# Gate projections with 512-column products, the dt step in four pieces, and a changed order of the output turns in a two-layer hybrid encoder

## The chip, the cores and the metric

One core of a Trainium2 chip runs the whole kernel. The metric is the device time of one execution in microseconds (us). The kernel before takes 1551.32 us (median of 3 runs, 1548.27 to 1552.07).

## The reference

Two layers work on 512 tokens of width 1024. Each layer is a mixer (a Mamba-2 state-space part beside windowed attention), an output projection, and a gated convolutional FFN. What the change touches:

```python
h = rms_norm(x, norm1_w[i])
proj = h @ w_in[i]
z, xbc, dt_raw, q, k, v = split(proj, ...)      # z: 1024 columns, 512 for each of 2 groups
dt = softplus(dt_raw + dt_bias[i])              # (L, 2 directions, 16 heads)
a_dt = dt * -exp(a_log[i])
a_cum = cumsum(a_dt)                            # inside each chunk of 128 tokens
decay = exp(a_cum[l] - a_cum[s])                # for l >= s; the other direction likewise
y_ssm = y_fwd + y_bwd + d_skip * xs
y_ssm = rms_norm(y_ssm * silu(z))               # per group of 512 columns
x = x + concat(y_ssm, y_attn) @ w_out[i]
```

All is fp32. The kernel splits each fp32 operand of a large product into a high and a low part (fp32r) and runs three products for one: high by high, high by low, low by high.

## The kernel before

Every large weight comes in units of up to 128 x 1024 elements. The list of units (L170 to L205) is the order of use. For each unit a DMA on the queue of SP fills one of 3 `raw` buffers (L141), ScalarE (ACT) copies the high part into one of 3 `whi` buffers (L161), and VectorE (DVE) subtracts it to give `wlo` (L162). `take` (L114) hands out a unit, and asks with high priority for the splits of three units ahead and the loads behind those. A `whi` buffer comes free when the last product that reads it is done.

One large product is three matmuls in `mm3` (L278 to L280). They write to 4 "dense" PSUM banks (`pd`, L98). Smaller products and transposes use 4 "small" banks (`psm`, L101). A planner orders the instructions of each engine when the program is built: it takes them in program order where they are ready by its own estimate of time, lets a later one go first on an engine that has nothing earlier ready, and puts `take` ahead. At run time each engine keeps that fixed order and waits on semaphores.

A layer's mixer goes as follows.

- **V and dt** (`vdt`, L496): 288 columns, into `v_sb` and `xdt`. The first layer's start (L509 to L538) is in an order written out by hand. The constants' transposes follow (`setup`, L266).
- **The dt step** (`dt_step`, L544, called at L610): the softplus as a chain of small VectorE instructions of 128 x 128 elements (L553 to L568), twelve products for the running sums (L581), their exponential `ex` (L582), a logarithm and an exponential on ScalarE (L586, L587), the copies `run` (L592), `own` (L593, L596), four transposes of `run` (L599), their copy (L601), a DMA to `sums` in DRAM (L602), and `sd` (L603, L604). Its tiles lie in a pool of their own that closes behind it (L611).
- **K** (L628), then ten dense pieces (L981): the state inputs `bc`, the queries `q`, the inputs `xa` and `xb`. `x_done` and `bc_done` run a convolution of 7 taps over two dense banks (L389, L395). Attention steps are mixed in between by `Side` (L400): each yield of a dense piece adds a credit, and a whole credit runs one step.
- **The gate** (`g_z`, L832, called for both groups at L993 and L994): per half of 256 columns it takes two units at once (4 contraction tiles each), and for each pair of token tiles fills one dense bank with 48 matmuls of 256 columns, then one Silu (L848) and a yield. That is 4 yields a group, and 192 matmuls.
- **The state-space steps** (`ssd_steps`, L853): 11 steps and 4 turns a group. A step fetches rows of `sums` by a DMA from POOL's queue (L898, 3 `rows` buffers), updates states (L875 to L882), forms decays on ScalarE and VectorE (L906 to L911), and multiplies (L922, L937). `outer` multiplies the result by `sz`, the gate. A turn scales and transposes one chunk (L955 to L962). The first group's steps and turns are mixed into the gate and the output projection, then the second group's.
- **The output projection** (`g_out`, L1008): two halves of 512 columns. It takes all 4 dense banks at once, and one unit (2 contraction tiles by 512 columns) per yield. The first group's turns must stand ahead of its unit 4.

Of the kernel before, what the change touches and what calls it, by code (L numbers as in the profile page):

```python
# [7 lines left out]
F32 = mybir.dt.float32  # L8
F32R = mybir.dt.float32r
AF = mybir.ActivationFunctionType  # L10
# [36 lines left out]
def encoder_kernel(  # L47
# [30 lines left out]
    def pool(name, **kw):  # L78
        return tc.tile_pool(name=name, **kw)
# [13 lines left out]
    def nm(s):  # L93
        uid[0] += 1
        return f"{s}_{uid[0]}"
# [74 lines left out]
    for i in range(DEPTH):  # L170
# [17 lines left out]
        for g in range(GROUPS):  # L188
            for half in range(2):
                pair(f"z{g}{half}", [(512 * g + 256 * half, 256)])  # L190
# [279 lines left out]
    for i in range(DEPTH):  # L470
        side = Side()
        with ExitStack() as mix:
# [17 lines left out]
            dtx = ExitStack()  # L490
            dtp = dtx.enter_context(pool(f"dt_{i}", bufs=1, reuse_waits="tile"))
            run = dtp.tile([P, NT, 2, 16], F32, name=nm("run"))
            xdt = dtp.tile([P, NT, 32], F32, name=nm("xdt"))
# [49 lines left out]

            def dt_step():  # L544

                def et(name, shape, dt=F32):
                    return dtp.tile([P] + shape, dt, name=nm(name))

                sp_e = et("sp_e", [NT, 32])
                sp_w = et("sp_w", [NT, 32])  # L550
                sp_w2 = et("sp_w2", [NT, 32])
                sp_a = et("sp_a", [NT, 32])
# [7 lines left out]
                for n in (15, 13, 11, 9, 7, 5, 3):  # L560
# [4 lines left out]


                adt = sp_e
                V.scalar_tensor_tensor(  # L568
                    adt,
# [5 lines left out]
                )  # L575
                ps = small_bank()
                cum = ps[:, : 6 * 64].rearrange("p (n c h) -> p n c h", n=6, c=NT)
                for n, (m, o) in enumerate(
                    ((f(t_le), 0), (f(t_gt), 0), (f(t_ge), 16), (f(t_lt), 16), (ones, 0), (ones, 16))
                ):  # L580
                    mm(cum[:, n], m, adt[:, :, o : o + 16], start=True, stop=True)  # L581
                S.activation(ex, cum, AF.Exp)  # L582

# [6 lines left out]

                for d in range(2):
                    S.copy(run[:, :, d], cum[:, 2 * d])  # L592
# [4 lines left out]
                psr = small_bank()  # L597
                for c in range(NT):
                    turn128(psr[:32, c * P : (c + 1) * P], run[:, c].rearrange("p d h -> p (d h)"), ident)  # L599
                runT = dtp.tile([32, NT, P], F32, name=nm("runT"))  # L600
                V.tensor_copy(runT, psr[:32].rearrange("p (c l) -> p c l", c=NT))  # L601
                nc.gpsimd.dma_start(sums[i].rearrange("c r l -> r c l"), runT)  # L602
                V.tensor_tensor(sd[:, 0], ex[:, 1], dts[:, :, 0:16], ALU.mult)  # L603
                V.tensor_tensor(sd[:, 1], ex[:, 3], dts[:, :, 16:32], ALU.mult)  # L604
# [6 lines left out]
            dtx.close()  # L611
# [147 lines left out]
            def xbc(g, r):  # L759
# [16 lines left out]
                def bc_turn():  # L776
# [55 lines left out]
            def g_z(g, r):  # L832
                sz = act_tile(F32)
                r["sz"] = sz
                for half in range(2):
                    ws = [take((i, f"z{g}{half}", j)) for j in range(2)]
                    cs = slice(256 * half, 256 * half + 256)
                    for tp in range(2):
                        bank = dense_bank()
                        for t in (2 * tp, 2 * tp + 1):  # L840
                            o = bank[:, (t % 2) * 256 : (t % 2) * 256 + 256]
                            sl = slice(t * P, (t + 1) * P)
                            for kt in range(KT):
                                hv, lv = (w.rearrange("p (k c) -> p k c", k=4)[:, kt % 4] for w in ws[kt // 4])
                                ah, al = hT[kt // 4]
                                mm3(o, ah[:, kt % 4, sl], al[:, kt % 4, sl], hv, lv, kt == 0, kt == KT - 1)
                        flush()
                        S.activation(sz[:, 2 * tp : 2 * tp + 2, cs], bank.rearrange("p (t c) -> p t c", t=2), AF.Silu)  # L848
                        yield
# [3 lines left out]
            def ssd_steps(sp, g, r):  # L853
# [123 lines left out]
                return [lambda k=k: step(k) for k in range(-1, 10)] + [lambda c=c: turn(c) for c in range(NT)]  # L977
# [14 lines left out]
            side.steps += ssd_steps(sp, 0, r0)  # L992
# [10 lines left out]
            side.steps += ssd_steps(sp, 1, r1)  # L1003
# [151 lines left out]
```

## Time and profile before

| | |
|---|---|
| median of 3 runs | 1551.32 us |
| profiled execution | 1550.66 us |
| span of the profile | 1549.0 us |
| TensorE (PE) busy | 1508.9 us, 97% |
| VectorE (DVE) busy | 876.5 us, 57% |
| ScalarE (ACT) busy | 793.4 us, 51% |
| GpSimd (POOL) busy | 174.7 us, 11% |
| mean granted clock of TensorE | 0.994 |

A busy PE counts each matmul from its start to its modelled end, and neighbours overlap, so the start-to-start distance tells what one costs. A row of the timeline has start, duration, engine, line, operation, written tile and read tiles, shapes, count, and in brackets the idle time before it with what ended that. A row of the windows has, for a stretch, the busy time of PE, weight loads (PEld), DVE, ACT and POOL with the number of instructions, then the granted clock, the DMA share and GB/s.

### The profile page before, as it was taken

What the parts mean: (1) busy time and instruction counts of PE and PEld (TensorE: products, weight loads), DVE (VectorE), ACT (ScalarE), POOL (GpSimd) and SP (SyncE); (2) the same over time, 40 slices, a digit from 0 to 9 for tenths busy, and PEclk for the clock granted to TensorE, in tenths of its full rate; (3) what the DMA queues carried; (4) which work ended last, traced back from release to release, by engine and by line L of the source; (5) the groups of instructions that cost most, each with busy time, mean ns of one, the idle gap of its engine ahead of it and who ended that gap; (6) DMA issues with size and microseconds to landing.
All of it is one profiled execution on the core that took longest, in us unless ns stands there. A gap on an engine that the chain in (4) does not pass through costs nothing.

```text
span 1549.0 us, 20219 instructions
## 1 busy us (share of the span) xinstructions
PE 1508.9 (97%) x7680; PEld 1238.0 (80%) x7680; DVE 876.5 (57%) x1406; ACT 793.4 (51%) x1464; POOL 174.7 (11%) x246
## 2 busy tenths in 40 slices
PE   7999999999999999999999999999999999999997
PEld 5787778877788888888887777887778888888886
DVE  5676777776644444433367777777666434443333
ACT  4467988863543233322356779788435323332223
POOL 2000002423200000000010000053232000000002
PEclk9899999999999999999999999999999999999999
DMA  6532333453323333322343322355422333333231
GB/s 206 156 82 76 83 85 103 134 169 95 108 88 98 102 95 96 95 96 95 99 137 104 89 75 62 83 123 182 132 95 82 95 97 101 101 96 96 95 96 68
DMA packets 113080, 161.48 MB, mean 104 GB/s; under 512 B 7932, under 2 KB 90108, under 8 KB 112975
## 3 DMA queue, kind: packets, MB, share of 16 engines
q1 hardware_dynamic: 104756, 132.60, 27.7%
q0 software_dynamic: 7648, 27.50, 6.7%
q8 instruction: 60, 0.98, 0.3%
q14 instruction: 38, 0.30, 0.1%
q10 hardware_dynamic: 578, 0.10, 0.0%
HBM read 155.82 MB, written 8.55 MB: 106 GB/s over the span
## 4 chain that ended last, share of the span: by engine, by line
PE 86%; ACT 4%; DVE 3%; issue 3%; POOL 2%; DMA 2%; POOLq 0%; ACTq 0%; DVEq 0%
PE pd L280 22%; PE pd L278 22%; PE pd L279 22%; PE psm L278 3%; PE psm L279 3%; PE psm L280 3%; PE psm L690 2%; PE psm L680 2%; PE psm L922 1%; PE psm L646 1%; DMA rows<-sums 1%; PE psm L647 1%; PE psm L937 1%; ACT whi L161 1%; PE psm L314 1%
## 5 line engine op out<-in xcount | busy, mean ns | idle before, releaser
L278 PE MATMUL pd<-t,whi 128*128 128x512 f32 (+1 forms) x1088 | 419.5, 386 | 1.5 <-ACT whi L161 1.5
L280 PE MATMUL pd<-t,wlo 128*128 128x512 f32 (+1 forms) x1088 | 419.4, 386 | 0.4 <-DVE wlo L162 0.4
L279 PE MATMUL pd<-t,whi 128*128 128x512 f32 (+1 forms) x1088 | 418.9, 385 | 0.0
L162 DVE TENSOR_TENSOR wlo<-raw,whi 128x1024 fp32r<-128x1024 f32 (+1 forms) x214 | 260.5, 1221 | 241.3 <-ACT whi L161 241.0
L161 ACT CAST whi<-raw 128x1024 fp32r<-128x1024 f32 (+1 forms) x214 | 221.8, 1040 | 240.9 <-PE pd L279 213.6
L278 PEld LDWEIGHTS pd<-t,whi 128*128 128x128 f32 x1088 | 204.7, 188 | 40.8 <-ACT whi L161 1.7
L280 PEld LDWEIGHTS pd<-t,wlo 128*128 128x128 f32 x1088 | 204.7, 188 | 40.2 <-issue 1.5
L279 PEld LDWEIGHTS pd<-t,whi 128*128 128x128 f32 x1088 | 205.0, 188 | 38.3 <-issue 0.8
L278 PE MATMUL pd<-whi,t 128*128 128x256 f32 (+2 forms) x544 | 188.9, 347 | 0.0
L279 PE MATMUL pd<-wlo,t 128*128 128x256 f32 (+2 forms) x544 | 180.3, 331 | 4.0 <-DVE wlo L162 3.9
L280 PE MATMUL pd<-whi,t 128*128 128x256 f32 (+2 forms) x544 | 181.7, 334 | 0.7 <-DVE t L962 0.7
L279 PEld LDWEIGHTS pd<-wlo,t 128*128 128x128 f32 x544 | 103.9, 191 | 17.2 <-DVE wlo L162 4.6
L278 PEld LDWEIGHTS pd<-whi,t 128*128 128x128 f32 x544 | 103.9, 191 | 13.7 <-issue 3.8
L280 PEld LDWEIGHTS pd<-whi,t 128*128 128x128 f32 x544 | 103.8, 191 | 11.5 <-DVE t L962 1.6
L1097 ACT CAST ph<-t 128x512 fp32r<-128x512 f32 x40 | 24.9, 623 | 143.0 <-PE psm L279 132.5
L1098 DVE TENSOR_TENSOR pl<-t,ph 128x512 fp32r<-128x512 f32 x40 | 27.7, 692 | 114.8 <-ACT ph L1097 114.8
L395 DVE SCALAR_TENSOR_TENSOR sg<-pd,fprm,sg 128x511 f32<-128x511 f32 x88 | 65.9, 748 | 30.7 <-ACT sg L389 29.0
L648 DVE CUSTOM_DVE_ANT_0 s<-psm,bias,sink_all 128x256 f32<-128x256 f32 (+1 forms) x128 | 65.6, 547 | 21.2 <-PE psm L647 8.0
L662 ACT ACTIVATE s<-s,nm 128x257 f32<-128x257 f32 (+1 forms) x128 | 70.5, 554 | 3.3 <-DVE nm L659 3.1
L395 DVE SCALAR_TENSOR_TENSOR xT<-pd,cprm,xT 128x511 f32<-128x511 f32 (+2 forms) x96 | 66.6, 742 | 5.2 <-PE psm L680 4.3
L278 PE MATMUL pd<-whi,ph 128*128 128x512 f32 x176 | 68.9, 391 | 0.0
L279 PE MATMUL pd<-wlo,ph 128*128 128x512 f32 x176 | 68.7, 390 | 0.0
(205 smaller groups left out, 2181.1 us busy)
## 6 DMA issues: line engine op xcount, KB each, us to landing
raw<-in_w_up_dram SPq DMA_DIRECT2D x88, 512.0 KB
raw<-in_w_in_dram SPq DMA_DIRECT2D x52, 512.0 KB
raw<-in_w_down_dram SPq DMA_DIRECT2D x44, 512.0 KB
rows<-sums POOLq DMA_DIRECT2D x32, 512.0 KB, 5.8
raw<-in_w_out_dram SPq DMA_DIRECT2D x32, 512.0 KB
bias<-toep POOLq DMA_DIRECT2D x16, 384.0 KB, 4.0
raw<-in_w_in_dram SPq DMA_DIRECT2D x18, 256.0 KB
x<-in_x_dram SPq DMA_DIRECT2D x8, 512.0 KB
```

The source lines that it names most:

```text
L161: S.copy(hi[:, :used], raw[:, :used])
L162: V.tensor_tensor(lo[:, :used], raw[:, :used], f(hi[:, :used]), ALU.subtract)
L278: mm(o, lh, rh, start=start, stop=False)
L279: mm(o, lh, rl, start=False, stop=False)
L280: mm(o, ll, rh, start=False, stop=stop)
L395: V.scalar_tensor_tensor(dst[:, lo:hi], src[:, lo + d : hi + d], taps[k], dst[:, lo:hi], ALU.mult, ALU.add)
L648: V.tensor_tensor_reduce(out=s4[:, h, :w], in0=ps[:, :w], in1=it.bias[h // 2][:, h % 2, it.j0 : it.j1], scale=1.0, scalar=sink4[:, h : h + 1],
L662: S.activation(s4[:, h, : w + 1], s4[:, h, : w + 1], AF.Exp, bias=nm4[:, h : h + 1], accum_out=den[:, h : h + 1])
L680: turn128(ps[:, c : c + P], it.s4[:, h, b * P : (b + 1) * P], ident)
L690: mm(po[c * HD : (c + 1) * HD, :256], v_sb[:, it.k0 // P + b, it.g * HD : (it.g + 1) * HD], it.pts[b][:, c * 256 : (c + 1) * 256], start=( ...
L1097: S.copy(h, p_sb[kt])
L1098: V.tensor_tensor(l, p_sb[kt], f(h), ALU.subtract)
```

## The change

The gate's units become 2 contraction tiles by 512 columns, four of them a group. `g_z` takes all 4 dense banks, one unit per yield, and issues 24 matmuls of 512 columns per yield; the four Silus follow in the last of the four. There are still 4 yields a group, so every credit falls as before. The dt step keeps only the chain up to L568 where it was. The rest is cut into `dt_sums` (called behind the first query piece), `dt_rows` (behind the second) and `dt_own` (behind the third). Its tiles move into the mixer's pool, and the scratch tile `junk` has one buffer in place of two. `ssd_steps` returns steps and turns apart, and the first group's four turns stand one place later, behind the second group's first step, which holds one fetch of rows and nothing else.

```diff
-            for half in range(2):
-                pair(f"z{g}{half}", [(512 * g + 256 * half, 256)])
+            for j in range(4):
+                add_unit((i, f"z{g}", j), wi, 2 * j, 2, [(512 * g, 512)])
...
-            dtp = dtx.enter_context(pool(f"dt_{i}", bufs=1, reuse_waits="tile"))
-            run = dtp.tile([P, NT, 2, 16], F32, name=nm("run"))
+            run = ep.tile([P, NT, 2, 16], F32, name=nm("run"))
...
+            def dt_sums():
+                ps = small_bank()
+                cum = ps[:, : 6 * 64].rearrange("p (n c h) -> p n c h", n=6, c=NT)
...
+                    mm(cum[:, n], m, sp_e[:, :, o : o + 16], start=True, stop=True)
+                S.activation(ex, cum, AF.Exp)
+                for d in range(2):
+                    S.copy(run[:, :, d], cum[:, 2 * d])
+                V.tensor_tensor(sd[:, 0], ex[:, 1], dts[:, :, 0:16], ALU.mult)
+                V.tensor_tensor(sd[:, 1], ex[:, 3], dts[:, :, 16:32], ALU.mult)
+
+            def dt_rows():
+                psr = small_bank()
+                for c in range(NT):
+                    turn128(psr[:32, c * P : (c + 1) * P], run[:, c].rearrange("p d h -> p (d h)"), ident)
+                runT = ep.tile([32, NT, P], F32, name=nm("runT"))
+                V.tensor_copy(runT, psr[:32].rearrange("p (c l) -> p c l", c=NT))
+                nc.gpsimd.dma_start(sums[i].rearrange("c r l -> r c l"), runT)
+
+            def dt_own():
                 V.tensor_scalar(sp_w, dts, 1e-37, None, ALU.max)
...
-                        junk = ep.tile([P, P], F32, tag="junk", name=nm("junk"), bufs=2)
+                        junk = ep.tile([P, P], F32, tag="junk", name=nm("junk"), bufs=1)
...
-                for half in range(2):
-                    ws = [take((i, f"z{g}{half}", j)) for j in range(2)]
-                    cs = slice(256 * half, 256 * half + 256)
-                    for tp in range(2):
-                        bank = dense_bank()
...
-                        S.activation(sz[:, 2 * tp : 2 * tp + 2, cs], bank.rearrange("p (t c) -> p t c", t=2), AF.Silu)
-                        yield
+                banks = [dense_bank() for _ in range(NT)]
+                for j in range(4):
+                    hi, lo = take((i, f"z{g}", j))
...
+                    for t in range(NT):
+                        sl = slice(t * P, (t + 1) * P)
+                        for k in range(2):
+                            kt = 2 * j + k
+                            ah, al = hT[kt // 4]
+                            mm3(banks[t], ah[:, kt % 4, sl], al[:, kt % 4, sl], hv[:, k], lv[:, k], kt == 0, kt == KT - 1)
+                        if j == 3:
+                            S.activation(sz[:, t], banks[t], AF.Silu)
+                    flush()
+                    yield
...
-                return [lambda k=k: step(k) for k in range(-1, 10)] + [lambda c=c: turn(c) for c in range(NT)]
+                return [lambda k=k: step(k) for k in range(-1, 10)], [lambda c=c: turn(c) for c in range(NT)]
...
+            later = {1: dt_sums, 3: dt_rows, 5: dt_own}
             for n, gen in enumerate(dense):
                 side.run(gen, RATE_A if n > 1 else 0)
+                if n in later:
+                    later[n]()
...
-            side.steps += ssd_steps(sp, 1, r1)
+            steps1, turns1 = ssd_steps(sp, 1, r1)
+            side.steps += steps1[:1] + turns0 + steps1[1:] + turns1
```

## Rows read from the trace of the kernel before

**Rows 1.** The page: span, and the chain that ended last by engine.
```profile
span 1549.0 us, 20219 instructions
...
PE 86%; ACT 4%; DVE 3%; issue 3%; POOL 2%; DMA 2%; POOLq 0%; ACTq 0%; DVEq 0%
```

**Rows 2.** Windows: the first layer's dt step, and the DMAs ahead of it.
```profile
24.00:26.00 2.00, 2.00 (x13) 1.26 (x12) 1.66 (x6) 0.81 (x3) 0.14 (x1) 1.00 0.00 1
...
36.00:38.00 2.00, 0.00 (x0) 0.00 (x0) 1.78 (x7) 0.00 (x0) 0.00 (x0) 0.50 0.95 315
...
48.00:50.00 2.00, 2.00 (x8) 1.56 (x7) 0.46 (x1) 0.00 (x0) 1.82 (x5) 0.78 0.96 263
```

**Rows 3.** Timeline of PE, first layer, 34 to 49 us.
```profile
39.76 0.66 PE L581 MATMUL psm<-sp_e,t_le 128*128 128x64 f32 x2 [4.89 <-DVE sp_w L585]
...
44.06 0.79 PE L278 MATMUL pd<-t,whi 128*128 128x512 f32 x1 [1.51 <-ACT whi L161]
...
45.36 0.78 PE L279 MATMUL pd<-t,whi 128*128 128x512 f32 x1
...
46.79 0.63 PE L280 MATMUL pd<-t,wlo 128*128 128x512 f32 x1
...
48.50 0.58 PE L278 MATMUL pd<-t,whi 128*128 128x512 f32 x1
```

**Rows 4.** Timelines of ACT and DVE, first layer, 33 to 47 us.
```profile
34.21 1.28 ACT L586 ACT_TABLE_LOAD   x1
...
42.97 1.04 ACT L161 CAST whi<-raw 128x1024 fp32r<-128x1024 f32 x1
...
39.32 0.29 DVE L568 SCALAR_TENSOR_TENSOR sp_e<-dts,expa_all 128x128 f32<-128x128 f32 x1
...
44.04 1.23 DVE L162 TENSOR_TENSOR wlo<-raw,whi 128x1024 fp32r<-128x1024 f32 x1 [0.57 <-ACT whi L161]
```

**Rows 5.** Timeline of POOL, first layer, up to 60 us: attention's first small copies.
```profile
49.80 0.44 POOL L642 COPY s<-sink_all 128x4 f32<-128x4 f32 x3
```

**Rows 6.** Timeline of PE, second layer, 813.5 to 819.5 us.
```profile
814.67 0.43 PE L581 MATMUL psm<-sp_e,t_le 128*128 128x64 f32 x2 [0.51 <-DVE sp_e L568]
...
816.03 0.47 PE L280 MATMUL pd<-t,wlo 128*128 128x512 f32 x1
...
818.86 0.61 PE L599 MATMUL psm<-ident,run 128*32 128x128 f32 x4 [1.66 <-ACT run L592]
```

**Rows 7.** Groups by line and form on PE: one of the gate's three.
```profile
L278 PE MATMUL pd<-whi,t 128*128 128x256 f32 x256 | 74.8, 292 | 0.0
```

**Rows 8.** Timeline of PE: gate, then output projection, each pair nine products apart.
```profile
242.02 0.28 PE L278 MATMUL pd<-whi,t 128*128 128x256 f32 x1
...
243.10 0.28 PE L278 MATMUL pd<-whi,t 128*128 128x256 f32 x1
...
380.04 0.39 PE L278 MATMUL pd<-whi,t 128*128 128x512 f32 x1
...
382.08 0.39 PE L278 MATMUL pd<-whi,t 128*128 128x512 f32 x1
```

**Rows 9.** Windows, first layer: attention, then gate, then output projection.
```profile
90.00:231.00 141.00, 140.22 (x795) 109.10 (x795) 103.91 (x274) 117.09 (x265) 8.93 (x22) 1.00 0.28 78
...
231.00:306.00 75.00, 71.04 (x520) 62.44 (x519) 54.75 (x66) 62.16 (x122) 26.30 (x28) 1.00 0.42 114
306.00:392.00 86.00, 85.69 (x401) 67.78 (x400) 58.73 (x81) 43.84 (x104) 27.27 (x29) 1.00 0.49 147
```

**Rows 10.** Timeline, 285 to 289 us: the gate's longest wait.
```profile
288.51 0.39 PE L279 MATMUL pd<-wlo,t 128*128 128x256 f32 x1 [1.95 <-DVE wlo L162]
```

**Rows 11.** Timelines of PE and DVE, first layer, 229 to 246.7 us.
```profile
230.82 0.39 PE L280 MATMUL pd<-t,wlo 128*128 128x512 f32 x1
...
231.84 0.36 PE L278 MATMUL pd<-whi,t 128*128 128x256 f32 x1
...
235.74 7.98 DVE L395 SCALAR_TENSOR_TENSOR xT<-pd,cprm,xT 128x509 f32<-128x509 f32 x12 [2.17 <-PE psm L680]
```

More of the change, by code (lines that the diff above doesn't have):

```diff
@@ L489, in encoder_kernel @@
             sd = ep.tile([P, 2, NT, 16], F32, name=nm("sd"))
-            dtx = ExitStack()
-            dtp = dtx.enter_context(pool(f"dt_{i}", bufs=1, reuse_waits="tile"))
-            run = dtp.tile([P, NT, 2, 16], F32, name=nm("run"))
-            xdt = dtp.tile([P, NT, 32], F32, name=nm("xdt"))
+            run = ep.tile([P, NT, 2, 16], F32, name=nm("run"))
+            xdt = ep.tile([P, NT, 32], F32, name=nm("xdt"))
             vb = [dense_bank() for _ in range(NT)]
@@ L542, in encoder_kernel @@
                     vdt(t, j)
+            sp_e, sp_w, sp_w2, sp_a = (ep.tile([P, NT, 32], F32, name=nm("sp")) for _ in range(4))
             def dt_step():
[L546 to L552, printed above, removed]
                 V.scalar_tensor_tensor(sp_e, xdt, -1.0, xdt, ALU.mult, ALU.min)
@@ L564, in dt_step @@
                 V.scalar_tensor_tensor(dts, sp_a, 2.0, dts, ALU.mult, ALU.add)
-                adt = sp_e
                 V.scalar_tensor_tensor(
-                    adt,
+                    sp_e,
                     dts,
@@ L580, in dt_step @@
                 ):
-                    mm(cum[:, n], m, adt[:, :, o : o + 16], start=True, stop=True)
+                    mm(cum[:, n], m, sp_e[:, :, o : o + 16], start=True, stop=True)
                 S.activation(ex, cum, AF.Exp)
+                for d in range(2):
[10 more added lines that the diff above has]
+            def dt_own():
                 V.tensor_scalar(sp_w, dts, 1e-37, None, ALU.max)
@@ L589, in dt_step @@
                 V.scalar_tensor_tensor(sp_a, sp_w, -1.0, sp_a, ALU.add, ALU.add)
-                for d in range(2):
-                    S.copy(run[:, :, d], cum[:, 2 * d])
                 V.tensor_tensor(
@@ L596, in dt_step @@
                 V.tensor_tensor(own[:, :, 1], own[:, :, 1], own[:, :, 0], ALU.subtract)
[L597 to L604, printed above, removed]
             if i == 0:
@@ L610, in encoder_kernel @@
             dt_step()
-            dtx.close()
             mixA = []
@@ L834, in g_z @@
                 r["sz"] = sz
-                for half in range(2):
-                    ws = [take((i, f"z{g}{half}", j)) for j in range(2)]
-                    cs = slice(256 * half, 256 * half + 256)
-                    for tp in range(2):
-                        bank = dense_bank()
[L840 to L847, printed above, removed]
-                        S.activation(sz[:, 2 * tp : 2 * tp + 2, cs], bank.rearrange("p (t c) -> p t c", t=2), AF.Silu)
-                        yield
+                banks = [dense_bank() for _ in range(NT)]
+                for j in range(4):
+                    hi, lo = take((i, f"z{g}", j))
+                    hv = hi.rearrange("p (k c) -> p k c", k=2)
+                    lv = lo.rearrange("p (k c) -> p k c", k=2)
+                    for t in range(NT):
[8 more added lines that the diff above has]
+                    yield
             mixS = [None, None]
@@ L991, in encoder_kernel @@
             sp = spx.enter_context(pool(f"ssd_{i}", bufs=1, reuse_waits="tile"))
-            side.steps += ssd_steps(sp, 0, r0)
+            steps0, turns0 = ssd_steps(sp, 0, r0)
+            side.steps += steps0
             side.run(g_z(0, r0), RATE_S)
```

## The prediction

> **What bounds the kernel now.** I read the page first. The chain that ended last runs on PE for 86% of a span of 1549.0 us [rows 1], so time goes only where PE idles, where its clock is low, or where one of its products costs more than it must. The windows come next: PE idles almost only around the first layer's dt step, where the clock is also at 0.50, its lower level of 1.2 GHz [rows 2], and in the gate stretch, 71.04 us busy of 75 against 85.69 of 86 in the output projection behind it [rows 9]. The second layer repeats the gate stretch. The timelines then tell what PE waits for in both places, and what one product costs from start to start. The sum is made against the profiled execution, 1550.66 us, 0.66 us under the median.
>
> **The gate's products.** 192 matmuls of 256 columns a group, in 2 groups and 2 layers, are 768, as three groups of 256 show [rows 7]. Nine of them take 1.08 us (242.02 to 243.10), and nine matmuls of 512 columns in the same form 2.04 us (380.04 to 382.08) [rows 8], so one costs 0.120 us and the other 0.227. Then 768 x 0.120 = 92.2 us becomes 384 x 0.227 = 87.2 us, **5.0 us** off a PE that nothing else holds there. The rows are rounded to 0.01 us, which moves the difference of 0.013 us by 0.003 either way: bounds 3.8 and 6.1 us. The Trainium skill, page "TensorE: Matmul & The Clock Gate", section "Back-to-back issue gap", speaks against this: there an isolated matmul takes its columns at 2.4 GHz plus about 2.5 ns, so two of 256 columns take 218 ns and one of 512 takes 216 ns. By that estimate the 384 pairs would save 1.0 us, not 5.0. The trace disagrees (0.24 against 0.227 us), and it has the duration of the same thing, so 5.0 stands.
>
> **The gate's units.** Before, a half takes two units at once and holds both until its last bank. Of 3 `whi` buffers one is then free, and at each change of half the second new unit is split late: PE waits 1.95 us for `wlo` [rows 10], once a layer. After, a unit serves 24 products (5.4 us) and frees its buffer, with two more split ahead. The output projection already runs that way and idles 0.31 us in 86 [rows 9]. So the wait goes: 2 x 1.95 = **3.9 us**. Bounds: 0, if VectorE's queue is late for another reason, and 7.9 us, if all idle time of the stretch goes (2 x (75 - 71.04) [rows 9]). Each Silu is a load of ScalarE's table and mostly one back; fewer may be needed when four Silus stand together, but ScalarE is busy 62.16 of 75 us and PE does not wait on it directly, so I count 0.
>
> **The four banks.** This is the added wait. The gate's first product starts at 231.84, when `xb` has just ended (230.82), and the convolution that reads `xb`'s two banks ends at 235.74 + 7.98 = 243.7 [rows 11]. Before, the gate needs a bank at a time and the two free ones last past that. After, token tiles 2 and 3 wait for it. Tiles 0 and 1 can go on with the first three units, all split by then: 2 x 6 x 3 = 36 products of 0.227 = 8.2 us, to 240.0. The 3.7 us left are covered in part by the rest of attention's products, which PE runs in that stretch. I take 1.0 us a layer, **-2.0 us**. Bounds: 0 if the products of attention cover it, and 9.2 us a layer if tile 2 blocks the queue after 12 products (231.84 + 2.7 = 234.5 to 243.7). Behind the blocked products on PE stand all later ones, among them the state products that VectorE needs next. At the changes from group to group and into `g_out`, the first bank's Silu is issued three token tiles (4.1 us) ahead of the next use, and what it may wait for is a table load of 1.28 us [rows 4], so 0 there.
>
> **The dt step, first layer.** PE waits 4.89 us for the chain, runs the twelve sums, waits 1.51 us for K's first split, and has its first low product at 46.79, with the clock at the lower level until 48 to 50 us [rows 2, 3]. K's raw units had landed by 24 us, when the DMAs stood still (0.00 share) [rows 2], yet ScalarE splits them at 42.97 and VectorE at 44.04, behind the dt step's instructions in its queue [rows 4]. So the planner believes them late. That decides what the new place is worth: where it has nothing earlier ready on an engine it takes a later piece, and the trace shows that it reaches far. POOL's copies for attention's first three items stand at 49.80 [rows 5], though all three come behind the first query piece in the program, where the sums now go, and the third within the second one. PE, ScalarE and VectorE would stand idle after L568 in its plan, with the sums, the logarithm and `own` ready. I expect them in their old places, ahead of K's split. What does change is order among ready work: the four transposes between 44.06 and 45.36 [rows 3] yield to K. There 1.30 - 0.43 (one product at the lower clock) = 0.87 us comes back, and they cost up to 0.61 us later [rows 6]: **0.3 us**. If the pieces do stay away, VectorE reaches K's split at 39.61 instead of 44.04, and the low product comes at 40.8 instead of 46.79, 6.0 us earlier. Of that I take 1.2 us for six more products at the lower clock (46.79 to 48.50 is four [rows 3], so 0.43 against 0.227 us), and 1.36 (814.67 to 816.03) + 0.61 us for the sums and transposes that then run among the dense products [rows 6]: 2.8 us. If K's split also goes ahead of the chain, ScalarE's at 34.21, where a table load stands now, and VectorE's by 36.5 (1.04 + 1.23 later) [rows 4], PE never stops: 10.3 + 5 x 0.2 - 1.97 = 9.3 us. The low bound is 0.
>
> **The dt step, second layer.** K's products are ready here, so PE runs them ahead of the chain, but queue order makes it wait 0.51 us for L568 and 1.66 us for `run` [rows 6]. After, dense products have precedence. I take 1.66, **1.7 us**, and nothing for the first, since the next product needs a `wlo` that VectorE finishes at about the same time. Bounds 0 and 2.2.
>
> **What costs nothing.** The logarithm's two table loads (1.28 us each), if they fall into attention, lie in ScalarE's free time there, 117.09 busy of 141 us; PE is busy 140.22 [rows 9]. If that cover is gone they cost up to 2.6 us a layer. The `sums` DMA moves behind attention's bias loads on POOL's queue, and still long ahead of its readers, which come with the gate. One fetch of the second group goes ahead of four turns; a turn puts nothing on POOL's queue or on SP's, so only the turns move, by one credit, and they still end ahead of unit 4 of the output projection: 0. `junk` with one buffer is written by VectorE alone, in order: 0.
>
> **Sum.** 5.0 + 3.9 - 2.0 + 0.3 + 1.7 = 8.9 us: 1550.66 - 8.9 = **1541.8 us**.
>
> **The rivals.** About 0.3%, 4.65 us, is what a measurement of this kernel can tell from no change: faster is under 1546.7, slower over 1556.0.
>
> **K early**, and the gate dense: K no longer waits and all idle time of the gate goes. 9.3 + 2.2 + 5.0 + 7.9 = 24.4 us, **1526.3**. For it: K's data is there at 24 us. Against it: the planner's belief above.
>
> **The banks eat the units' gain.** Tiles 0 and 1 go ahead but nothing fills the 3.7 us: 8.9 + 2.0 - 7.4 = 3.5 us, **1547.2**. For it: the convolution's end at 243.7 is late and attention's tail is short.
>
> **The gate gains nothing.** Wider products cost two narrow ones, and VectorE's queue is as late as before: 0.3 + 1.7 = 2.0 us, **1548.7**. Against it: both distances are in the rows.
>
> **Four banks block PE**, the other side. If PE's queue holds tile 2 right behind the first 12 products, it stands 9.2 us a layer, and the clock falls as it did around the dt step, where PE was empty (0.00) and the clock 0.50 [rows 2]; some 11 products at 0.20 us more make 2.2 us. 2 x (9.2 + 2.2) = 22.8 us against gains of 10.9: **1562.6**. It decides from 5.5 us a layer on. Against it: the planner lets ready work past, as K's second bank shows, whose two high products stand between 45.36 and 46.79, ahead of the first bank's low one [rows 3]. The Trainium skill, the same page, section "A second HAM failure mode: psum-queue depth-cycling", tells of a kernel that idles between groups as it goes through PSUM banks and whose clock swings between both levels; by that rule this rival comes about. The trace does not agree so far: the gate stretch has 1.00 throughout [rows 9].
>
> **How the numbers follow.** My forecast has 0.50, K early 0.13, banks that eat the gain 0.17, no gain in the gate 0.09, blocked PE 0.11. The range 1529 to 1549 holds the forecast, the two small cases and the middle ground towards the fastest; it leaves out the blocked case and about half of the fastest, 0.18. Faster: 0.50 + 0.13 and a third of the third case, 0.69. Slower: 0.11. Same: 0.20.
>
> **What would show it.** Gate products 0.227 us apart, 384 of them; no wait on `wlo` of about 2 us in the gate; in the first layer the sums still ahead of K near 40 us and the clock at 0.50 until about 49 us; in the second no wait of the transposes on `run`. The forecast is wrong if PE waits over 2 us a layer at the gate's start, if K's first low product comes before 45 us, or if attention's stretch grows by more than 2 us.

## The result, and the profile after

The changed kernel takes 1566.57 us (median of 4 runs, 1565.01 to 1569.23); the kernel before, beside it on the same chip, 1551.69. The ratio is 1.0097, interval 1.008 to 1.0113: it is slower by about 15 us. The forecast was 1541.8 us with a range up to 1549. The profiled execution took 1567.12 us. Its page, answering to [rows 1]:

```profile
span 1565.4 us, 19426 instructions
...
PE 84%; DMA 4%; issue 4%; ACT 3%; DVE 3%; POOL 2%; POOLq 0%; SPq 0%; ACTq 0%; DVEq 0%
```

The span grew by 16.4 us, and PE's share of the chain fell from 86 to 84%. DMA rose from 2 to 4%, 3 of it the fetches of `rows`. The windows, answering to [rows 9], and two short ones around the end of the gate:

```profile
231.00:306.00 75.00, 68.36 (x324) 51.05 (x322) 52.20 (x65) 55.95 (x118) 27.33 (x26) 0.98 0.39 108
306.00:392.00 86.00, 82.85 (x356) 64.42 (x356) 52.30 (x69) 40.76 (x96) 25.05 (x26) 0.94 0.46 128
...
300.00:305.00 5.00, 1.12 (x4) 0.72 (x4) 3.03 (x4) 4.97 (x10) 3.62 (x4) 0.80 0.00 0
305.00:310.00 5.00, 3.78 (x12) 2.87 (x12) 2.83 (x5) 1.25 (x3) 1.08 (x2) 0.50 0.63 189
```

PE idles more in both stretches, and behind the gate's end its clock is at 0.50, the lower level of 1.2 GHz, which before only the dt step had shown [rows 2]. From 300 to 305 us PE works 1.12 of 5 us and ScalarE 4.97. The second layer repeats this. From `xb`'s last product to the output projection's last it now takes 183.0 us in the first layer (229.98 to 412.98) and 183.1 in the second, where it took 174.5 (230.82 to 405.30) and 175.0: 16.6 us, so the whole loss lies in these two stretches. The timeline of PE, first layer (line numbers are the changed kernel's: L574 the sums, L955 the turns' transposes, L918 the products with `em`):

```profile
39.20 0.66 PE L574 MATMUL psm<-sp,t_le 128*128 128x64 f32 x2 [4.91 <-DVE sp L593]
...
45.38 0.63 PE L280 MATMUL pd<-t,wlo 128*128 128x512 f32 x1
...
239.04 0.39 PE L278 MATMUL pd<-whi,t 128*128 128x512 f32 x1
...
241.08 0.39 PE L278 MATMUL pd<-whi,t 128*128 128x512 f32 x1
...
297.73 0.39 PE L280 MATMUL pd<-whi,t 128*128 128x512 f32 x1
...
298.81 1.03 PE L955 MATMUL psm<-ident,t 128*128 128x128 f32 x8
303.11 1.12 PE L955 MATMUL psm<-ident,t 128*128 128x128 f32 x4 [3.26 <-DVE yo L935]
305.91 1.97 PE L918 MATMUL psm<-t,em 128*128 128x64 f32 x8 [1.69 <-DVE em L907]
307.64 0.77 PE L278 MATMUL pd<-whi,t 128*128 128x512 f32 x1
...
332.52 0.60 PE L955 MATMUL psm<-ident,t 128*128 128x128 f32 x4
...
339.37 0.50 PE L278 MATMUL pd<-whi,t 128*128 128x512 f32 x1 [2.14 <-ACT t L957]
...
340.75 0.79 PE L280 MATMUL pd<-whi,t 128*128 128x512 f32 x1 [0.65 <-DVE t L958]
```

The gate's last product starts at 297.73 and the output projection's first at 307.64. Between them stand the transposes of three turns and the eight products of one `em`, in PE's fixed order, with two waits. Further on, unit 4 of the output projection waits for the fourth turn. In the kernel before, the two products stood 1.47 us apart and the fourth turn's transposes came earlier:

```profile
303.44 0.28 PE L280 MATMUL pd<-whi,t 128*128 128x256 f32 x1
...
304.91 0.80 PE L278 MATMUL pd<-whi,t 128*128 128x512 f32 x1
...
323.06 0.60 PE L959 MATMUL psm<-ident,t 128*128 128x128 f32 x4
```

ScalarE in the changed kernel's stretch (L902 adds `own` to the fetched rows, L843 is the gate's Silu, L905 the decays' exponential, L941 the square that ends a chunk of state steps, L1000 the cast of attention's output, which the output projection reads first, L957 a turn's copy):

```profile
294.49 1.29 ACT L902 ACTIVATE rows<-rows,own 128x128 f32<-128x128 f32 x4 [2.54 <-DMA rows<-sums]
295.80 1.28 ACT L843 ACT_TABLE_LOAD   x1
297.09 0.60 ACT L843 ACTIVATE t<-pd 128x512 f32<-128x512 f32 x1
297.70 1.28 ACT L905 ACT_TABLE_LOAD   x1
...
299.31 0.61 ACT L941 ACTIVATE y<-t 128x512 f32<-128x512 f32 x1
...
301.85 1.28 ACT L843 ACT_TABLE_LOAD   x1
303.15 1.57 ACT L843 ACTIVATE t<-pd 128x512 f32<-128x512 f32 x3
304.60 1.15 ACT L1000 CAST t<-x 128x512 fp32r<-128x512 f32 x2
...
310.12 3.21 ACT L1000 CAST t<-x 128x512 fp32r<-128x512 f32 x6
...
336.32 0.41 ACT L902 ACTIVATE rows<-rows,own 128x128 f32<-128x128 f32 x1 [3.20 <-DMA rows<-sums]
...
338.74 0.58 ACT L957 CAST t<-psm 128x512 fp32r<-128x512 f32 x1
```

ScalarE waits 2.54 us for rows, changes its table three times for four Silus, and comes to the casts only at 304.60. At 336.32 it waits 3.20 us for rows again, and the fourth turn's copy stands behind that wait. In the kernel before, the same square came at nearly the same time, and the first casts came before the gate had ended:

```profile
299.72 0.63 ACT L945 ACTIVATE y<-t 128x512 f32<-128x512 f32 x1 [1.85 <-DVE t L943]
...
300.64 1.12 ACT L1000 CAST t<-x 128x512 fp32r<-128x512 f32 x2
```

PE's two waits in the changed kernel, 3.26 and 1.69 us, name VectorE. GpSimd and VectorE there show what stands behind them (L287 and L289 make a chunk's scale from its square, L951 multiplies by it):

```profile
300.10 0.19 POOL L287 TENSOR_SCALAR ms<-gss 128x1 f32<-128x1 f32 x1 [3.50 <-ACT y L941]
...
301.97 0.49 DVE L951 TENSOR_SCALAR t<-t,rs 128x512 f32<-128x512 f32 x1 [3.46 <-POOL rs L289]
...
304.10 1.75 DVE L907 TENSOR_TENSOR em<-rows,cb 128x512 f32<-128x512 f32 x1
```

GpSimd waits for ScalarE's square, VectorE waits for GpSimd's scale, and only then come the third turn, `yo` and `em` in VectorE's queue, although ScalarE had been through with the decays at 301.83. So PE stood for a chain of three engines that begins in ScalarE's queue. The square itself came 0.8 us after its operand (L939, over at 298.51), behind a table load: most of the wait is the chain's own length, which in the kernel before the gate's products covered until 303.44. The last Silu was over at 304.72 and the first casts at 305.75, so PE could not have gone on before about 305 us for these either.

### The profile page after: what moved, and what is told of

It reads as the page before. It is cut to its first block, busy times and chain, and to the rows that moved or that the text cites. A ratio compares the mean times of both kernels' runs of the same rounds, so it can differ in the third digit from the quotient of the medians.

```text
span 1565.4 us, 19426 instructions
## 1 busy us (share of the span) xinstructions
PE 1515.4 (97%) x7296; PEld 1222.0 (78%) x7296; DVE 873.3 (56%) x1406; ACT 784.2 (50%) x1456; POOL 182.0 (12%) x246
## 4 chain that ended last, share of the span: by engine, by line
PE 84%; DMA 4%; issue 4%; ACT 3%; DVE 3%; POOL 2%; POOLq 0%; SPq 0%; ACTq 0%; DVEq 0%
PE pd L280 21%; PE pd L278 21%; PE pd L279 21%; PE psm L280 3%; PE psm L279 3%; PE psm L278 3%; DMA rows<-sums 3%; PE psm L686 2%; PE psm L676 2%; PE psm L918 1%; PE psm L642 1%; PE psm L876 1%; PE psm L643 1%; DMA bias<-toep 1%; PE psm L933 1%
## 5 line engine op out<-in xcount | busy, mean ns | idle before, releaser
L278 PE MATMUL pd<-whi,t 128*128 128x512 f32 (+1 forms) x416 | 170.3, 409 | 4.3 <-ACT t L957 4.2
L280 PE MATMUL pd<-whi,t 128*128 128x512 f32 (+1 forms) x416 | 160.1, 386 | 2.0 <-DVE t L958 1.3
L279 PE MATMUL pd<-wlo,t 128*128 128x512 f32 (+1 forms) x416 | 158.8, 382 | 0.1
L278 PEld LDWEIGHTS pd<-whi,t 128*128 128x128 f32 x416 | 80.0, 192 | 24.6 <-ACT t L957 6.3
L280 PEld LDWEIGHTS pd<-whi,t 128*128 128x128 f32 x416 | 79.8, 192 | 19.3 <-DVE t L958 2.7
L279 PEld LDWEIGHTS pd<-wlo,t 128*128 128x128 f32 x416 | 79.9, 192 | 18.1 <-issue 4.8
L395 DVE SCALAR_TENSOR_TENSOR xT<-pd,cprm,xT 128x509 f32<-128x509 f32 (+2 forms) x96 | 67.5, 744 | 3.3 <-ACT xT L389 3.2
```

Source lines behind the costliest of these rows:

```text
L278: mm(o, lh, rh, start=start, stop=False)
L279: mm(o, lh, rl, start=False, stop=False)
L280: mm(o, ll, rh, start=False, stop=stop)
L395: V.scalar_tensor_tensor(dst[:, lo:hi], src[:, lo + d : hi + d], taps[k], dst[:, lo:hi], ALU.mult, ALU.add)
```

## The experiments

Every run stands beside runs of the kernel before on its own chip (medians 1550.45 to 1551.81 us), so the ratio is the measure; 0.1% is 1.55 us. "dt", "gate" and "turns" are the three parts of the change.

| run | kernel | median us | ratio, 95% interval |
|---|---|---|---|
| e1 | before + gate | 1560.13 | 1.0053, 1.004 to 1.0065 |
| e2 | before + turns | 1555.30 | 1.0024, 1.0014 to 1.0034 |
| e3 | before + dt | 1547.85 | 0.9973, 0.9962 to 0.9984 |
| e4 | changed, old turns (gate + dt) | 1557.68 | 1.0039, 1.0027 to 1.0051 |
| e5 | e3 + first group's gate wide | 1556.59 | 1.0036, 1.0023 to 1.0048 |
| e6 | e3 + second group's gate wide | 1553.01 | 1.0012, 1.0002 to 1.0021 |
| e7 | e1, no Silu | 1550.92 | 0.9998, 0.9988 to 1.0008 |
| e8 | e1, casts earlier | 1549.30 | 0.9983, 0.9974 to 0.9992 |
| e9 | e4, casts earlier | 1548.66 | 0.9985, 0.9974 to 0.9997 |
| e10 | changed, casts earlier | 1559.16 | 1.0051, 1.0033 to 1.0068 |
| e11 | e9, steps given out more slowly | 1561.73 | 1.0066, 1.005 to 1.0082 |
| e12 | e3, steps given out more slowly | 1553.85 | 1.0016, 1.0006 to 1.0027 |
| e13 | e9, four `rows` buffers | 1540.18 | 0.9932, 0.9916 to 0.9947 |
| e14 | e3, four `rows` buffers | 1544.75 | 0.996, 0.9946 to 0.9973 |
| e15 | e9, products in halves | 1554.42 | 1.0023, 1.0013 to 1.0032 |
| e16 | e13, more casts earlier | 1550.17 | 0.9996, 0.9986 to 1.0006 |
| e17 | changed, four `rows` buffers | 1552.55 | 1.0002, 0.9991 to 1.0013 |
| e18 | e4, four `rows` buffers | 1549.26 | 0.9984, 0.9972 to 0.9995 |

**Which part costs: e1 to e4.** Each takes hunks of the change as they are. e1:

```diff
-                pair(f"z{g}{half}", [(512 * g + 256 * half, 256)])
+                add_unit((i, f"z{g}", j), wi, 2 * j, 2, [(512 * g, 512)])
```

> The kernel before with the gate's edit alone (units of 512 columns, four banks). In the changed kernel the stretch from the gate's first product to the output projection's last took about 6 us a layer more, where I had counted 3.5 us less. Theory A (the gate's edit makes the loss between gate and output projection: Silus and steps bunch up behind a faster PE, banks and turns come late): the stall of some 8 us a layer ahead of the output projection's first product stays, the one ahead of its unit 4 (2.3 + 0.8 us a layer) goes; 2 x (6.0 - 3.1) = 6 us slower than before, about 1557. Theory B (the turns' new place makes both stalls, the gate's edit is as I counted it): 2 x 3.5 = 7 us faster, about 1544.

e2, against before:

```diff
-            side.steps += ssd_steps(sp, 1, r1)
+            side.steps += steps1[:1] + turns0 + steps1[1:] + turns1
```

> The kernel before with the first group's turns behind the second group's first step, and nothing else. Theory A: the fourth turn is issued just ahead of unit 4 whatever the gate does, so the output projection waits 2 to 3 us a layer there: 4 to 7 us slower, 1555 to 1558. Theory B: both stalls, some 10 us a layer less what the gate had won: 1565 or more. Theory C (with the narrow gate the turns have time enough, the stall needs a faster gate): no change, 1550 to 1552.

e3, against before:

```diff
+            later = {1: dt_sums, 3: dt_rows, 5: dt_own}
```

> The kernel before with the dt step cut in four and its tiles in the mixer's pool, and nothing else. By the milestones of the changed kernel's trace it brought 0.8 us in the first layer up to the end of xb, and cost 0.6 us in the second: 1549 to 1552. As I had predicted it: 2.0 us faster, 1549. If its new order on POOL's queue (scores copied behind the sums DMA) is what hurts: slower, 1553 or more.

e4, against the changed kernel:

```diff
-            side.steps += steps1[:1] + turns0 + steps1[1:] + turns1
+            side.steps += ssd_steps(sp, 1, r1)
```

> The changed kernel with the turns back in their old place. Theory A: the wait ahead of unit 4 (2.3 + 0.8 us a layer) and some of the low clock behind it go, the stall ahead of the output projection stays: 6 to 8 us faster than the changed kernel, 1559 to 1561. Theory B: both stalls go: 1544 or less. Theory C: as A.

The gate costs 0.53%, some 8 us, where I had counted 6.9 us of gain; the turns cost 0.24%, some 4 us, where I had counted 0; the dt step gains 0.27%, some 4 us. Theory A holds in direction, B and C fall. The gate alone is dearer than A had it, e4 comes out some 1 to 3 us faster than A said, and the dt step is worth more. The parts do not add up: alone they make +0.50%, together +0.97%. Most of the rest lies between turns and gate, since the turns cost 0.58% (1.0097 against 1.0039) beside the wide gate. The timeline of PE in e2 shows the turns' wait with the narrow gate:

```profile
334.25 0.50 PE L278 MATMUL pd<-whi,t 128*128 128x512 f32 x1 [1.73 <-ACT t L961]
```

**Where in the gate: e5 and e6.** The unit list and `g_z` in the new form for one group alone:

```diff
-            side.run(g_z(0, r0), RATE_S)
+            side.run(g_wide(0, r0), RATE_S)
```

> The kernel with the dt step's edit alone (1547.85), and the first group's gate alone in units of 512 columns; the second group's stays narrow. Theory S (the loss is made at the gate's end: the second group's four Silus all come in its last unit, behind ScalarE's wait for rows, and the output projection needs their banks and the casts behind them): the second group's end is as it was, so the products' gain stays without the loss, 2 x 1.25 us for 192 pairs: about 1545. Theory P (a PE that is faster than the state steps beside it stands wherever the work of the gate ends): it only arrives earlier by 1.25 us a layer and loses it there: 1547 to 1549, or slower still if the banks of the group change cost.

> The same with only the second group's gate in units of 512 columns. Theory S: the whole loss, about what the gate's edit cost with the dt edit in place (1557.68 against 1547.85) and up to 2 us more or less: 1556 to 1560. Theory P: about half of it, 1551 to 1554.

A miss for theory S: the first group alone costs more (0.63% over e3) than the second (0.39%), and nearly as much as both (0.66%, e4 over e3). So the four Silus of the second group are not the one cause. Theory P fits better: e6 is in its range, but e5 is 8 us above the range that P gave it, which P had left open upward. In e5 PE stands at the same place, the gate's end, and for `em` (in e6 there too, 3.21 us for the cast):

```profile
304.31 1.09 PE L941 MATMUL psm<-t,em 128*128 128x64 f32 x4 [3.09 <-DVE em L930]
```

**What is late there: e7 and e8.** e7 replaces the gate's function by a plain copy, which the result then lacks; e8 moves half of the casts (`cast_mix` holds the body of the loop over `b`):

```diff
-                            S.activation(sz[:, t], banks[t], AF.Silu)
+                            S.activation(sz[:, t], banks[t], AF.Identity)
```

> The kernel before with the gate's edit alone (1560.13), and a plain copy on ScalarE in place of the gate's Silu; the gate's function is left out of the result. Theory T (two table loads in front of and between the second group's four Silus, 2 x 1.28 us and one back, are what makes them late): the output projection's first product comes up to 4 us a layer earlier, 1552 to 1555. If ScalarE's wait for rows and the casts behind decide: within 3 us of 1560.

```diff
                     flush()
+                    if g and j == 1:
+                        cast_mix(0)
                     yield
...
-            for b in range(2):
+            cast_mix(1)
```

> The kernel before with the gate's edit alone (1560.13), and the first half of the casts of attention's output (high part L1000, low part L1001) issued behind the second unit of the second group's gate, ahead of its Silus. Theory C (PE stands at the output projection because its operand is cast too late, 304.6 to 315 us): the first half's operands are there when the gate ends, PE stands only for the first Silu's bank or the turns, 303 at the latest instead of 307.6, and the low clock behind is shorter: 4 to 6 us a layer, 1548 to 1552. Theory B2 (the banks, behind the Silus, decide): first product at about 303 to 304 only if PE's queue is not held by turns and em; 1555 to 1560.

Both give back what the gate's edit had cost: 0.55% under e1, a little more than T had said, and 0.70%, as C had said. `cast_mix` also brings VectorE's low casts forward. In e7 the first product comes at 303.81, 3.8 us sooner than in e1, as T had said, and waits 1.80 us for the cast. In e8 it stands right behind the gate, and turns and `em` come among the output projection's products:

```profile
300.10 0.39 PE L280 MATMUL pd<-whi,t 128*128 128x512 f32 x1
...
300.78 0.80 PE L278 MATMUL pd<-whi,t 128*128 128x512 f32 x1
...
305.71 1.10 PE L934 MATMUL psm<-t,em 128*128 128x64 f32 x8 [1.61 <-DVE em L923]
```

So the loss hangs on ScalarE's queue at the gate's end: with less in it (e7), or with the casts further forward in it (e8), the loss is gone. In both, the turns' transposes no longer stand ahead of the first product in PE's queue either, and no run parts the two. Nor does e7 show that table loads are what the change added: the kernel before has seven of them around the same four Silus (276 to 305 us), the changed kernel three, and no run takes Silu out of the narrow gate. And e8 is only 0.17% faster than the kernel before, where products and units had promised 8.9 us. The next runs ask why.

**Adding up and pacing: e9 to e12.** e9 is e4 with e8's edit, e10 the changed kernel with it. e11 and e12 change the credits:

```diff
-            side.run(g_z(0, r0), RATE_S)
-            side.run(g_z(1, r1), RATE_S)
+            side.run(g_z(0, r0), 1.2)
+            side.run(g_z(1, r1), 1.2)
...
-                side.run(g_out(half), RATE_S)
+                side.run(g_out(half), 1.6)
```

> The changed kernel with the turns in their old place and the first half of the casts ahead of the second group's Silus, so e8 with the dt step's edit. If the edits add up: e8's 1549.3 less what the dt edit brought beside the wide gate (1560.13 - 1557.68 = 2.4) or alone (3.7): 1545.6 to 1547. If the dt edit's gain was the same time as the casts' (a shorter way to the gate's end): 1549.

> The changed kernel with the first half of the casts ahead of the second group's Silus and nothing else. The turns' new place cost 3.7 us alone and 1566.57 - 1557.68 = 8.9 us beside the wide gate. If the wide gate makes it dearer only by the stall ahead of the output projection: 3.7 us over e9, about 1550. If a PE that is through the gate sooner always meets the fourth turn that much too early: 8 to 9 us over e9, about 1555.

> e9 with the state steps given out more slowly beside the gate (a credit of 1.2 in place of 1.4 a yield) and faster beside the output projection (1.6). In e8 PE still waits for em four times, 1.31 + 0.90 + 1.17 + 1.78 = 5.2 us a layer, and that is where the products' 2.5 us a layer went. If em's products stand in PE's queue only because the steps are given out too early: 3 to 5 us a layer come back, 1537 to 1541. If the chain of the state steps itself is the limit (VectorE, ScalarE, GpSimd and the rows' DMA in turn): the wait moves behind the gate or to the output projection's end, 1545 to 1550.

> The kernel with the dt step's edit alone (1547.85) with the same pace of 1.2 and 1.6. In its trace PE waits for em 1.5 us and for wlo 2.0 us in the gate. If pace is worth only what em waits show: 1545 to 1548. If later turns come too late for unit 4: 1549 or more.

In e9 nothing of the dt step's gain shows; its interval covers e8's. e10 is 0.66% over e9, so the turns' new place costs more where PE comes early than alone (0.24%). ScalarE's timeline in e10 tells why: the fourth turn's copy (L969) stands behind a wait for rows again.

```profile
332.32 0.99 ACT L914 ACTIVATE rows<-rows,own 128x128 f32<-128x128 f32 x3 [3.48 <-DMA rows<-sums]
...
335.61 0.57 ACT L969 CAST t<-psm 128x512 fp32r<-128x512 f32 x1
```

e11 is a miss: slower steps did not save the waits for `em` (4.2 us in the first layer, in e9 4.3) and cost time. PE waits 3.3 us for one `em` and 2.8 us for the fourth turn. e12 loses 0.43% to e3, as its second alternative says: it waits for no `em`, but 2.4 us for the fourth turn. So in both the state steps, given out more slowly in the gate, bring the fourth turn too late.

**The chain of the state steps: e13 to e16.** The waits of e9 in the gate and at its end (engine, line, what for: total, times, longest):

```profile
POOL rows L906 <- DVE em L919: 11.7, 7, 6.2
...
PE psm L930 <- DVE em L919: 4.3, 5, 1.6
```

GpSimd may not fetch new rows until an `em` has read the old ones. e13 and e14:

```diff
-                    rw = sp.tile([P, 2, 4, P], F32, tag="rows", name=nm("rows"), bufs=3)
+                    rw = sp.tile([P, 2, 4, P], F32, tag="rows", name=nm("rows"), bufs=4)
```

> e9 with four buffers for the rows in place of three. In e9's gate GpSimd waits 11.7 us for em in seven places before it may fetch the next rows, ScalarE 1.9 us for the rows and PE 4.3 us for em. Theory R (the chain of the state steps is held by the rows' buffers): the fetch goes out a step sooner, PE's waits for em of 4.3 us a layer go for the most part, 1540 to 1543. Theory V (it is held by the order of VectorE's and ScalarE's queues, in which the next row's work stands behind the last): no change, 1547 to 1550.

> The kernel with the dt step's edit alone (1547.85) with four buffers for the rows. Theory R: its PE waits 1.5 us a layer for em in the gate, so 1545 to 1547. Theory V: no change, 1547 to 1549.

e15 cuts every gate product in two:

```diff
-                            mm3(banks[t], ah[:, kt % 4, sl], al[:, kt % 4, sl], hv[:, k], lv[:, k], kt == 0, kt == KT - 1)
+                            for c in (0, 256):
+                                cs = slice(c, c + 256)
+                                mm3(
+                                    banks[t][:, cs], ah[:, kt % 4, sl], al[:, kt % 4, sl], hv[:, k, cs], lv[:, k, cs],
+                                    kt == 0 and not c, kt == KT - 1 and c > 0,
+                                )
```

> e9 with each gate product cut in two of 256 columns, everything else (units, banks, Silus, casts) as there: 768 products of 0.120 us again in place of 384 of 0.227 us. If the width gains what I counted, and PE is what decides in the gate: 5 us slower than e9, 1553 to 1555. If the state steps decide and PE only waits the longer for em (4.3 us a layer in e9): the 2.5 us a layer come out of those waits, 1547 to 1550, and PE's waits for em shrink to some 2 us a layer.

e16 (`cast_hi` holds the high casts alone):

```diff
+                    if g and j == 2:
+                        his.append(cast_hi(1))
```

> e13 with the high casts of the second half too ahead of the Silus. ScalarE has then 2.2 us less to do between the Silus and the output projection. If what is left of the low clock and of PE's waits around 300 to 310 us (some 2 us a layer) hangs on ScalarE: 2 to 3 us faster than e13; if on em alone: as e13.

Theory R has the time: e13 is 0.53% faster than e9 and, at 1540.18 us, faster than both kernels. It has the mechanism in part, as PE's waits for `em` fall by a third and not for the most part. In the profiles 6.0 of the 8.9 us lie from `xb` to the output projection's end; the rest lies between these stretches of the two layers, where no rows are fetched, and is not explained. The same two rows in e13, then its ScalarE at the gate's end:

```profile
POOL rows L906 <- DVE em L919: 8.4, 3, 5.6
...
PE psm L930 <- DVE em L919: 2.9, 3, 1.2
```

```profile
294.68 1.28 ACT L853 ACT_TABLE_LOAD   x1
295.97 0.60 ACT L853 ACTIVATE t<-pd 128x512 f32<-128x512 f32 x1
297.46 0.60 ACT L853 ACTIVATE t<-pd 128x512 f32<-128x512 f32 x1 [0.89 <-PE pd L280]
...
299.61 0.59 ACT L853 ACTIVATE t<-pd 128x512 f32<-128x512 f32 x1
...
301.14 0.59 ACT L853 ACTIVATE t<-pd 128x512 f32<-128x512 f32 x1
```

The four Silus take one table load, and PE is busy for all of 300 to 310 us with the clock at 1.00:

```profile
300.00:305.00 5.00, 5.00 (x26) 3.93 (x25) 4.51 (x6) 5.00 (x13) 2.59 (x3) 1.00 0.71 215
305.00:310.00 5.00, 5.00 (x26) 4.12 (x25) 5.00 (x7) 3.83 (x8) 1.60 (x1) 1.00 0.72 206
```

Whether the fourth buffer helps the narrow gate too is not shown: e14 is 0.13% under e3, within their intervals. e15 is 0.38% over e9, 5.9 us (3.5 to 8.3 by the intervals), where I had said 5.0. That is a balance and not the width alone: PE's waits change with it (2.3 us for a Silu, which e9 does not have, less for `em`), and the time between the two layers' stretches is 3.5 us shorter. The timeline of PE has nine of its halves in 1.08 us, as [rows 8]:

```profile
283.77 0.28 PE L278 MATMUL pd<-whi,t 128*128 128x256 f32 x1
...
284.85 0.28 PE L278 MATMUL pd<-whi,t 128*128 128x256 f32 x1
```

e16 is a miss by 10 us. The casts now stand among the state steps' bias adds and exponentials in ScalarE's queue, all before 290 us, from 300 to 305 us PE's clock is at 0.69 on average, and PE waits longer for `em` from 231 to 306 us than e13's 2.9 us. That is 3.4 us more in two layers; the rest is not traced:

```profile
PE psm L938 <- DVE em L927: 4.6, 4, 1.9
```

**Rows or casts: e17 and e18.** The edit of e13 in the changed kernel and in e4.

> The changed kernel with four buffers for the rows and nothing else. If the fetch that goes out a step sooner also frees ScalarE ahead of the Silus (2.5 us of waiting for rows in the changed kernel's trace), the stall ahead of the output projection shrinks and the late fourth turn is left: 1566.6 less some 8 us, 1556 to 1560. If the casts behind the Silus hold PE whatever the rows do: 1563 to 1567.

> The changed kernel with the turns in their old place (e4, 1557.68) and four buffers for the rows; the casts stay late. It tells how much of e13 is the rows' buffers alone. If the casts are needed too: 1549 to 1553. If the rows are enough: within 2 us of e13's 1540.2.

The fourth buffer alone takes 0.94% off the changed kernel, more than said, and 0.55% off e4. ScalarE's waits for rows from 231 to 345 us fall from 10.7 us in the changed kernel to 6.1 in e17, and GpSimd's for a free buffer from 231 to 306 us from 11.0 to 7.0; GpSimd also makes the turns' scales, so the gain may come by either queue. In e17's first layer the wait for the fourth turn is gone, and what holds the output projection now is the cast itself, as in e18:

```profile
303.37 0.50 PE L278 MATMUL pd<-whi,t 128*128 128x512 f32 x1 [1.73 <-ACT t L1000]
...
306.42 0.80 PE L278 MATMUL pd<-whi,t 128*128 128x512 f32 x1 [1.36 <-ACT t L1000]
```

So the two edits each take a part: e18 with the casts moved as well is e13, 0.52% faster. In e17's second layer the fourth turn still costs 0.9 and 0.7 us.

## Why the prediction was wrong

**The gate's products: right.** Nine of them take 241.08 - 239.04 = 2.04 us, and nine halves 1.08 us in e15, so a pair of halves costs 13 ns more, 5.0 us for 384 pairs. e15 over e9 measured 5.9 us, with other waits in it. The Trainium skill's estimate by "TensorE: Matmul & The Clock Gate", section "Back-to-back issue gap", which is for isolated products, made it 2.5 ns; the stream of products here disagrees with it, as the rows had.

**The gate's units: right as a wait, worth nothing as a term.** No `wlo` wait stands in the gate's rows any more. The 3.9 us were given back at once: PE waits longer for `em` instead (from 231 to 345 us 3.4 us in the first layer, in four places, and 3.3 in the second, where before it was 1.5 in each).

**The four banks at the start: wrong, on the safe side.** I charged 2.0 us. The gate's first 45 products run from 233.47 to 243.57 without a gap, and PE waits for no bank. The convolution ends at 241.69, 2.0 us sooner than before, just when the 36 products that I had counted for tiles 0 and 1 are through. In e1, where the gate starts at 230.19, PE does wait 0.4 us for it. The rival of blocked PE came nearest in time (1562.6 against 1566.6), but its place is not where the time went.

**The failing step: "so 0 there", at the change into `g_out`.** I took the Silu of the first bank as the only thing the output projection waits for, and left ScalarE out since "PE does not wait on it directly". PE does, directly or through other engines, at one place. The gate's dense work now ends at 298 us, 5.7 us sooner than before (the last gate product started at 303.44, now at 297.73), while the state steps are no further: ScalarE's square of the third chunk comes at 299.31, before at 299.72. From then on PE has only what these steps let through, and at the lower clock behind it: the first product comes 9.9 us after the gate's last, where it was 1.47. In the changed kernel the way is ScalarE's square, GpSimd's scale, VectorE's turn and `em`. In e6, e7, e17 and e18 it is the cast, which PE waits for by name, and in e15 a Silu's bank (2.31 us). The sum had -6.9 us for the gate's edit; e1 measured +0.53%, about 15 us off. That the loss is made by the gate's edit is shown by e1, and that it goes when the casts come forward by e8, or when ScalarE has no Silu by e7. That the wait for rows' buffers is part of it at both places is shown by e17 and e18, where one more buffer takes 0.94% and 0.55% off and, in e17's first layer, the fourth turn's wait with it; that both edits are needed for e13's time is shown by e9 and e18. Each of these edits also makes the planner order the stretch anew, so no run moves one instruction alone: how much of the loss is ScalarE's lateness and how much the place of turns and `em` ahead of the first product in PE's queue stays open, and so does why e5 costs more than e6.

**The turns: wrong.** The term "they still end ahead of unit 4 of the output projection: 0" counted a credit as no time. With the first fetch ahead of it the fourth turn is given out right before unit 4; its transposes run at 332.52 (in the kernel before, at 323.06) and its copy waits in ScalarE's queue behind rows. It costs 0.24% alone, 0.58% beside a PE that arrives sooner. A place in the program that had just enough slack was taken for one with any amount.

**The dt step: right in its steps, a little small.** The sums stay in their old place (39.20 us), and K's first low product comes at 45.38, later than the 45 us that I had named as the bound; K early did not happen. In the second layer the transposes no longer wait for `run`. I counted 2.0 us; e3 gives 0.27%, 2.5 to 5.9 us by its interval. The span of its profile, 1546.6 us, is 2.4 us under that of before: 0.9 us by the end of the first layer's output projection, where I had counted 0.3, and 1.5 more by the end of the second layer's `xb`, where I had counted 1.7.

**The sum.** 5.0 us were there; 3.9 were swapped for another wait, and the gate's end and the fourth turn were priced at 0. With the casts ahead, the turns back and a fourth buffer (e13) the wide gate does come out 0.28% under the narrow one with a fourth buffer (e14), about 4.3 us; a narrow gate with the casts moved was not run, so that is not the width's gain alone.

## What to carry to other kernels

Where a dense stretch covers a chain of small steps, its length is also the time that chain has: before making the dense work shorter, ask at its end what the next dense work reads, which queue makes it, and what that queue waits for. Follow that through every engine: here PE's wait named VectorE and began in ScalarE's queue. A fetch whose buffer is freed by its own consumer can set the pace of such a chain: one buffer more took 0.53% off the wide gate with early casts (e13 under e9), and nothing clear of noise off the narrow one (e14 under e3). A step that moves by only one credit has to be followed to the instruction that reads its result.

## What the runs showed that I had not expected

The fetch of rows takes a median of 5.8 us from issue to landing in e9, as before, and ScalarE's waits for it from 231 to 345 us grew from 5.5 us before to 10.7 us in the changed kernel; in e9 they are 3.6. They do not decide alone: in e7 they are 16.2 us, and e7 is 0.55% faster than e1, which has 9.6. The clock fell with PE's empty stretch: 0.80 in the 5 us in which PE was busy for 1.12 us, 0.50 in the next 5, in which it was busy for 3.78. And moving half of the casts ahead of the Silus gained 0.70% (e8 under e1), while moving the other half's high casts there as well lost 0.64% (e16 over e13).
